# A longer row pitch for the activation tiles of a one-core transformer block kernel

## The chip, the cores and the metric

The kernel runs on one core of a Trainium2 chip. The metric is device time in microseconds (us) of one execution, the median of several; lower is better.

## The reference

One layer of a block on 256 positions with width 2048, in float32. Only what shapes the kernel is kept here:

```python
z = x @ w_in[i] + b_in[i]                       # 2048 -> 6 x 2048: u, v, a, b, gate A, gate B
zu, zv, za, zb, zga, zgb = jnp.split(z, IN_SPLITS, axis=-1)
sg = spatial_gating(gelu(zu), gelu(zv), ...)    # layer norm of v, 8 groups, 128-position blocks
y_a = sg @ w_gm_out[i]
c = causal_depthwise_conv(za * sigmoid(zb), cv_w[i], cv_b[i])      # 31 taps
c = silu(layer_norm(c, ...)); y_b = c @ w_cv_out[i]
mix = (sigmoid(zga) * y_a + sigmoid(zgb) * y_b) @ w_o[i]
x = layer_norm(ALPHA * x + mix, ...)
idx, gate = peer_route(xf, peer_wq[i], peer_keys[i])     # 8 heads, top 16 of 128 x 128 keys
u = jnp.take(u_tab, ib, axis=0); h = einsum('tkd,td->tk', u, xb)   # 16384 experts
v = jnp.take(v_tab, ib, axis=0); y = einsum('tk,tkd->td', gb * gelu(h), v)
x = layer_norm(ALPHA * x + y, ...)
x = x + sigmoid(x @ ple_w_gate[i]) * (p[i] @ ple_w_proj[i])
```

## The kernel before

Every product is done by TensorE in a split form: a float32 operand is cut into a high part (`hi`, rounded to the type fp32r by ScalarE) and a low part (`lo`, the rest, made by VectorE), both in `split` (L101 to L103). Activations are kept split and transposed, contraction on the partitions: `xT`, `mT`, `x1T` (one after another in the one buffer of pool `act`) and `sgT`, `cT` (pool `s32`) are tiles of 16 rows per partition, one row for each contraction tile `kt`. A row has 512 elements of 4 bytes, 2048 bytes: 256 high parts, then 256 low parts.

Weights come from memory as `raw` tiles of 128 x 1024 (512 KB, L131), in one fixed order, and are split into `hi` and `lo`. Two of them make a unit.

- `prod_t` (L147 to L171) is the product with the result transposed. The weights are stationary, and the row `x[:, kt, :]` streams as the moving operand. For each half of the contraction there are 8 matmuls of 512 columns with `hi` (L155) and 8 of 256 columns with `lo` (L159), each with a weight load of its own. It issues high 0 to 7 and low 0 to 7 for the first half, high 8 to 14, low 8 to 15 and high 15 for the second. So a unit is 32 matmuls in runs of 8 or 9 high, 8 low, 7 high, 8 low. It is called 80 times with `xT`, 16 with `sgT`, 16 with `cT`, 144 with `x1T` (16 for the router's queries, 128 for all experts' first layer).
- `prod_n` (L181 to L207) is the product with positions on the partitions. Here 128 columns of `x` are the stationary operand and 512 columns of `hi` or `lo` stream (L195). It runs with `xT` (v), `mT` (w_o) and `x2T` (last gate).
- The experts' second layer (L798) has `ahl`, the split activation of the experts, as stationary operand, and `hi` or `lo` streams, 512 columns each time.

All experts are computed densely, and the router's result is laid over them as a table of gates (L728). The order on each engine is the order in which the code is written, with VectorE's side work (convolution, norms, routing) taken from a queue `side` between halves of a unit.

Tiles get their places in order of allocation in pools, and `pad` tiles (L70 to L75) only take up room ahead of a pool. The byte offsets of the tiles inside a partition, as the built program has them, stand under the change.

Of the kernel before, what the change touches and what calls it, by code (L numbers as in the profile page):

```python
# [10 lines left out]
F32R = mybir.dt.float32r  # L11
# [5 lines left out]
P = 128  # L17
D = 2048
T = 256
KT = D // P  # L20
# [8 lines left out]
ALPHA = 2.0 ** 0.25  # L29
EPS = 1e-5  # L30
EARLY = 64
NEG = -3.0e38
RATES = {"ab": 3.1, "v": 3.0, "u": 3.6, "ga": 2.6, "wa": 3.0}
ROUTE_RATE = 1.0
# [4 lines left out]
def block_kernel(ctx: ExitStack, tc: tile.TileContext, a: dict, out: bass.AP):  # L39
    nc = tc.nc  # L40

    def pool(stack, name, bufs=1, **kw):
        return stack.enter_context(tc.tile_pool(name=name, bufs=bufs, **kw))
# [3 lines left out]
    const = pool(ctx, "const")  # L47
    sp = pool(ctx, "stream")
    ev = pool(ctx, "evac", bufs=2)
    act = pool(ctx, "act")  # L50
# [19 lines left out]
    def pad(p_, nbytes):  # L70

        t = p_.tile([P, nbytes // 4], F32, name="pad")
        nc.gpsimd.memset(t[:, 0:1], 0.0)

    pad(const, 608)  # L75

    class InOrder:

# [185 lines left out]
    pc = pool(pa, "pa_const")  # L264
    s32 = pool(pa, "s32", bufs=2)
    s16 = pool(pa, "s16", bufs=3)

    xT = act.tile([P, KT, 2 * T], F32R, tag="act", name="xT")
    def load_x(q):
        raw = sp.tile([P, 1024], F32, tag="raw", name="rawx", bufs=4)  # L270
        nc.sync.dma_start(raw, a["xT"][q])
        rv = raw.rearrange("p (k t) -> p k t", k=4)
        split(rv, xT[:, q * 4:q * 4 + 4, :T], xT[:, q * 4:q * 4 + 4, T:])
# [156 lines left out]
    cT = s32.tile([P, KT, 2 * T], F32R, tag="s32", name="cT")  # L430
    csum = pc.tile([P, T], F32, tag="cacc", name="csum", bufs=2)
    crs = pc.tile([P, T], F32, name="crs")
    pad(pc, 256)
    ct1 = pc.tile([P, T], F32, tag="cacc", name="ct1", bufs=2)
    Q = 4

# [56 lines left out]
    flush()  # L493


    mT = act.tile([P, KT, 2 * T], F32R, tag="act", name="mT")
    for ct in range(KT):
        ps = prod_t(cT)
        y = join_t(ps)
# [34 lines left out]
    ped = dram.tile([P, NB, D], F32, name="ped")  # L534
    with tc.issue_after(last_dma[0].ins):
        nc.sync.dma_start(ped, pe)
    x1T = act.tile([P, KT, 2 * T], F32R, tag="act", name="x1T")
    ln1.finish(x1T)
    x1d = dram.tile([P, NB, D], F32, name="x1d")
    with tc.issue_after(last_dma[0].ins):  # L540
# [6 lines left out]
    op_ = pool(pg, "oh", bufs=3)  # L547
    ga1 = pool(pg, "ga1").tile([P, EARLY, T], F32, name="ga1")
    pr = ctx.enter_context(ExitStack())
# [15 lines left out]
    def top8_first(vdst, idst, src, scr):  # L565
        paced.max(vdst[:, 0:8], src)
        paced.max_index(idst[:, 0:8], vdst[:, 0:8], src)
        paced.match_replace(scr, vdst[:, 0:8], src, NEG)

# [123 lines left out]
    def ga_parts(lo_, hi_):  # L693
        if lo_ < min(hi_, EARLY):
            yield ga1[:, lo_:min(hi_, EARLY), :], lo_
        if max(lo_, EARLY) < hi_:
            yield now["ga2"][:, max(lo_, EARLY) - EARLY:hi_ - EARLY, :], max(lo_, EARLY)

# [13 lines left out]
    while side:  # L712
        u_unit(i2, ROUTE_RATE)
        i2 += 1
    assert i2 <= EARLY
    pr.close()
# [209 lines left out]
```

## Time and profile before

| | us |
|---|---|
| median of 3 runs | 2523.0 (2522.11 to 2524.18) |
| the profiled execution, its time | 2522.61 |
| its span, first to last instruction | 2520.8 |
| TensorE (PE) busy | 2491.0 (99%) |
| weight loads (PEld) busy | 2143.3 (85%) |
| VectorE (DVE) busy | 1902.8 (75%) |
| ScalarE (ACT) busy | 1263.8 (50%) |

The profiled execution has 1.8 us outside its span, and is 0.4 us below the median. Matmuls overlap each other in the pipeline, so a matmul's own duration in a row is longer than the step from its start to the next one's start; where the text speaks of a matmul's step, it means the latter. Weight loads run beside the matmul ahead of them. The mean granted clock of TensorE was 0.998 of 2.4 GHz.

### The profile page before, as it was taken

The numbers are of one execution on the slowest core, as the hardware profiler recorded it, in microseconds if no ns is written. First come the engines' busy times: TensorE is split into PE (matmuls) and PEld (weight loads), VectorE is DVE, ScalarE is ACT, GpSimd is POOL, SyncE is SP. The second block draws the span as 40 slices with busy tenths as digits, with TensorE's granted clock in tenths as the row PEclk, the third lists the DMA queues.
The fourth block names the chain that finished last, engine by engine and source line by source line (L and its number), as shares of the span: only waits on it lengthen the run. The fifth ranks groups of instructions, "written<-read, shape, count | busy, mean of one in ns | idle before, by whom it ended". The sixth has DMA issues, their size and how long they took to land.

```text
span 2520.8 us, 35685 instructions
## 1 busy us (share of the span) xinstructions
PE 2491.0 (99%) x13178; PEld 2143.3 (85%) x13178; DVE 1902.8 (75%) x3550; ACT 1263.8 (50%) x1922; POOL 12.1 (0%) x16
## 2 busy tenths in 40 slices
PE   8999999999999999999999999999999999999989
PEld 7888888888888788888888888888888888888877
DVE  6999999999765689988777888755665565555585
ACT  5444555447543545455444444545555544555553
POOL 0000000000000000000000000000000000000000
PEclk9999999999999999999999999999999999999999
DMA  7656555556566655555554455557676666666655
GB/s 239 242 184 199 185 192 176 178 175 216 188 194 193 232 176 185 190 184 184 167 161 164 160 167 167 168 188 254 200 225 195 193 194 195 193 193 193 194 190 175
DMA packets 130335, 482.15 MB, mean 191 GB/s; under 512 B 14832, under 2 KB 15472, under 8 KB 128240
## 3 DMA queue, kind: packets, MB, share of 16 engines
q1 hardware_dynamic: 129024, 476.11, 58.9%
q10 hardware_dynamic: 1136, 3.76, 0.4%
q8 instruction: 103, 1.69, 0.3%
q14 instruction: 72, 0.59, 0.1%
HBM read 473.52 MB, written 6.29 MB: 190 GB/s over the span
## 4 chain that ended last, share of the span: by engine, by line
PE 94%; DVE 4%; ACT 1%; issue 1%; DMA 0%; POOL 0%; SPq 0%; DVEq 0%; POOLq 0%; ACTq 0%
PE pst L155 35%; PE py L798 27%; PE pst L159 18%; PE psn L195 10%; PE pgate L728 2%; DVE lo L103 2%; ACT hi L102 1%; DVE cacc L82 1%; PE ptr L249 0%; PE pss L606 0%; PE pmix L402 0%; DVE ct L446 0%; DMA rawx<-in_xT 0%; PE ppe L531 0%; DVE x1N L82 0%
## 5 line engine op out<-in xcount | busy, mean ns | idle before, releaser
L103 DVE TENSOR_TENSOR lo<-raw,hi 128x1024 fp32r<-128x1024 f32 x864 | 1056.8, 1224 | 428.6 <-ACT hi L102 423.3
L102 ACT ACTIVATE hi<-raw 128x1024 fp32r<-128x1024 f32 x868 | 917.7, 1058 | 559.4 <-PE py L798 336.4
L155 PE MATMUL pst<-x1T,hi 128*128 128x512 f32 x2304 | 603.1, 399 | 3.2 <-DVE x1T L103 2.6
L798 PE MATMUL py<-hi,ahl 128*128 128x512 f32 x2048 | 506.6, 389 | 0.0
L155 PEld LDWEIGHTS pst<-x1T,hi 128*128 128x128 f32 x2304 | 413.6, 189 | 75.8 <-DVE x1T L103 3.5
L798 PEld LDWEIGHTS py<-hi,ahl 128*128 128x128 f32 x2048 | 384.5, 188 | 79.7
L155 PE MATMUL pst<-xT,hi 128*128 128x512 f32 x1280 | 328.3, 396 | 9.2 <-ACT hi L102 8.1
L159 PEld LDWEIGHTS pst<-x1T,lo 128*128 128x128 f32 x2304 | 314.3, 190 | 23.8
L159 PE MATMUL pst<-x1T,lo 128*128 128x256 f32 x2304 | 321.1, 282 | 0.0
L155 PEld LDWEIGHTS pst<-xT,hi 128*128 128x128 f32 x1280 | 232.0, 190 | 51.5 <-ACT hi L102 8.7
L798 PE MATMUL py<-lo,ahl 128*128 128x512 f32 x1024 | 274.6, 389 | 0.0
L175 ACT ACTIVATE e<-pst 128x256 f32<-128x256 f32 x160 | 61.5, 384 | 356.1 <-PE pst L155 356.1
L798 PEld LDWEIGHTS py<-lo,ahl 128*128 128x128 f32 x1024 | 192.2, 188 | 40.1 <-DVE lo L103 0.3
L82 DVE SCALAR_TENSOR_TENSOR cacc<-glu,cvw,cacc 128x256 f32<-128x256 f32 x464 | 197.3, 479 | 0.0
L159 PEld LDWEIGHTS pst<-xT,lo 128*128 128x128 f32 x1280 | 175.0, 191 | 17.2 <-DVE lo L103 4.9
L159 PE MATMUL pst<-xT,lo 128*128 128x256 f32 x1280 | 179.7, 283 | 2.8 <-DVE lo L103 2.8
L178 DVE TENSOR_TENSOR z<-pst,e 128x256 f32<-128x256 f32 x224 | 93.9, 419 | 70.9 <-ACT e L175 70.5
L175 ACT ACTIVATE e<-pst,binT 128x256 f32<-128x256 f32 x80 | 37.8, 472 | 169.6 <-PE pst L155 165.9
L725 DVE TENSOR_SCALAR oh<-iota,T,TG 128x128 f32<-128x128 f32 x256 | 87.7, 343 | 44.6 <-PE pgate L728 44.6
L103 DVE TENSOR_TENSOR ahl<-ga,ahl 128x256 fp32r<-128x256 f32 x256 | 106.9, 418 | 0.2 <-ACT ahl L102 0.2
L102 ACT ACTIVATE ahl<-ga 128x256 fp32r<-128x256 f32 x256 | 102.1, 399 | 1.6 <-DVE ga L736 1.6
L728 PE MATMUL pgate<-oh 128*128 128x128 f32 x512 | 78.9, 274 | 0.0
(290 smaller groups left out, 1799.7 us busy)
## 6 DMA issues: line engine op xcount, KB each, us to landing
raw<-in_peer_u SPq DMA_DIRECT2D x256, 512.0 KB, 3.4
raw<-in_peer_v SPq DMA_DIRECT2D x256, 512.0 KB, 5.0
raw<-in_wa SPq DMA_DIRECT2D x32, 512.0 KB, 3.4
raw<-in_wb SPq DMA_DIRECT2D x32, 512.0 KB, 3.4
raw<-in_wv SPq DMA_DIRECT2D x32, 512.0 KB, 3.4
raw<-in_wu SPq DMA_DIRECT2D x32, 512.0 KB, 3.4
raw<-in_wga SPq DMA_DIRECT2D x32, 512.0 KB, 3.3
raw<-in_w_gm_out SPq DMA_DIRECT2D x32, 512.0 KB, 3.3
```

Source lines behind the costliest of these rows:

```text
L82: return lambda *args, **kw: tc.keep_in_program_order(op(*args, **kw))
L102: nc.scalar.activation(hi, src, AF.Copy)
L103: eng.tensor_tensor(lo, src, hi.bitcast(F32), op=OP.subtract)
L155: nc.tensor.matmul(ps, hi[:, k * P:(k + 1) * P], x[:, kt, :], start=(kt == 0), stop=(kt == KT - 1))
L159: nc.tensor.matmul(ps[:, T:], lo[:, k * P:(k + 1) * P], x[:, half * 8 + k, :T], start=False, stop=False)
L175: nc.scalar.activation(e1, ps[:, T:], AF.Identity, bias=bias)
L178: nc.vector.tensor_tensor(z, ps[:, :T], e1, op=OP.add)
L195: nc.tensor.matmul(ps[b], x[:, kt, j * T + b * P:j * T + (b + 1) * P], w[:, k * 512:(k + 1) * 512], start=(kt == 0 and not is_lo and j == ...
L725: nc.vector.tensor_scalar(oh[:, 0, :], iota, T1[:, t:t + 1], TG[:, t:t + 1], op0=OP.is_equal, op1=OP.mult)
L728: nc.tensor.matmul(now["ps"][:, j * P:(j + 1) * P], oh[:, 0, :], oh[:, 1, :], start=True, stop=True)
L798: nc.tensor.matmul(py[b][half * 2 + k], ahl[:, j * T + b * P:j * T + (b + 1) * P], w[:, k * 512:(k + 1) * 512], start=(i2 == 0 and not is_ ...
```

## The change

The tiles `xT` and `mT` get rows of 520 elements (2080 bytes) and `x1T` rows of 514 (2056 bytes); of each row the first 512 are used, through a slice. The pad ahead of the streaming pool shrinks by 512 bytes, so that the pool `act`, now 512 bytes larger, ends where it ended. The pad in `pc` shrinks by 224 bytes.

```diff
+PITCH = 2 * T + 8
...
-    pad(const, 608)
+    pad(const, 96)
...
-    xT = act.tile([P, KT, 2 * T], F32R, tag="act", name="xT")
+    xT = act.tile([P, KT, PITCH], F32R, tag="act", name="xT")[:, :, :2 * T]
...
-    pad(pc, 256)
+    pad(pc, 32)
...
-    mT = act.tile([P, KT, 2 * T], F32R, tag="act", name="mT")
+    mT = act.tile([P, KT, PITCH], F32R, tag="act", name="mT")[:, :, :2 * T]
...
-    x1T = act.tile([P, KT, 2 * T], F32R, tag="act", name="x1T")
+    x1T = act.tile([P, KT, 2 * T + 2], F32R, tag="act", name="x1T")[:, :, :2 * T]
```

No instruction is added, removed or moved: on all five engines the built programs have the same rows in the same order (TensorE 4131 rows of equal neighbours, VectorE 2932, ScalarE 1756, GpSimd 19, SyncE 83), and only the line numbers behind the new line are one higher. What differs is places, in bytes inside a partition:

| tile | before | after | modulo 512 before, after |
|---|---|---|---|
| `raw`, 4 buffers | 18432 + 4096 n | 17920 + 4096 n | 0, 0 |
| `hi`, `lo`, 2 buffers each; weights of step k at + 512 k | 34816 + 4096 n | 34304 + 4096 n | 0, 0 |
| `xT`, `mT` row kt | 55296 + 2048 kt | 54784 + 2080 kt | 0, 32 kt |
| `x1T` row kt | 55296 + 2048 kt | 54784 + 2056 kt | 0, 8 kt |
| `cT` row kt | 113664 + 2048 kt | 113440 + 2048 kt | 0, 288 |
| `sgT` row kt | 146432 + 2048 kt | 146208 + 2048 kt | 0, 288 |
| `ahl`, 3 buffers | 91648 + 2048 n | the same | 0, 0 |
| `x2T` row kt | 88064 + 2048 kt | the same | 0, 0 |

The tiles of `s16` (`vN`, `uT`, `sA`, `sB`, `zN`) move by 224 bytes like `sgT`; those of `evac` move by 512; `glu`, the expert tables and the routing tiles stay.

## Rows read from the trace of the kernel before

**Rows 1.** The page: the span, TensorE's busy time and its granted clock.
```profile
span 2520.8 us, 35685 instructions
...
PE 2491.0 (99%) x13178; PEld 2143.3 (85%) x13178; DVE 1902.8 (75%) x3550; ACT 1263.8 (50%) x1922; POOL 12.1 (0%) x16
...
PEclk9999999999999999999999999999999999999999
```

**Rows 2.** The chain of work that ended last, by engine and line.
```profile
PE 94%; DVE 4%; ACT 1%; issue 1%; DMA 0%; POOL 0%; SPq 0%; DVEq 0%; POOLq 0%; ACTq 0%
```

**Rows 3.** Waits of TensorE, the longest: us in total, times, longest.
```profile
PE pst L155 <- ACT hi L102: 8.7, 4, 7.0
PE ptr L249 <- DVE x1N L241: 6.3, 1, 6.3
```

**Rows 4.** Groups of TensorE by line and shape: busy us, mean ns, idle before.
```profile
L155 PE MATMUL pst<-x1T,hi 128*128 128x512 f32 x2304 | 603.1, 399 | 3.2 <-DVE x1T L103 2.6 <-ACT hi L102 0.6
L798 PE MATMUL py<-hi,ahl 128*128 128x512 f32 x2048 | 506.6, 389 | 0.0
L155 PE MATMUL pst<-xT,hi 128*128 128x512 f32 x1280 | 328.3, 396 | 9.2 <-ACT hi L102 8.1 <-DVE xT L103 1.1
L159 PE MATMUL pst<-x1T,lo 128*128 128x256 f32 x2304 | 321.1, 282 | 0.0
...
L159 PE MATMUL pst<-xT,lo 128*128 128x256 f32 x1280 | 179.7, 283 | 2.8 <-DVE lo L103 2.8
...
L155 PE MATMUL pst<-sgT,hi 128*128 128x512 f32 x256 | 64.4, 393 | 0.0
...
L195 PE MATMUL psn<-hi,xT 128*128 128x512 f32 x256 | 63.2, 389 | 0.0
```

**Rows 5.** Timeline of TensorE, one unit with `x1T`: start us, us.
```profile
1031.59 1.12 PE L159 MATMUL pst<-x1T,lo 128*128 128x256 f32 x8
1032.55 1.78 PE L155 MATMUL pst<-x1T,hi 128*128 128x512 f32 x7
1034.16 1.11 PE L159 MATMUL pst<-x1T,lo 128*128 128x256 f32 x8
1035.11 2.23 PE L155 MATMUL pst<-x1T,hi 128*128 128x512 f32 x9
1037.18 1.11 PE L159 MATMUL pst<-x1T,lo 128*128 128x256 f32 x8
```

**Rows 6.** Timeline of TensorE in the experts' second layer.
```profile
1800.03 1.07 PE L798 MATMUL py<-lo,ahl 128*128 128x512 f32 x4
1800.94 1.98 PE L798 MATMUL py<-hi,ahl 128*128 128x512 f32 x8
1802.75 1.07 PE L798 MATMUL py<-lo,ahl 128*128 128x512 f32 x4
```

**Rows 7.** Single lines of the kernel: duration ns min/median/max, first and last start us.
```profile
L159 PE MATMUL pst<-sgT,lo x256: 277/283/283, 465.6 to 552.8; 128*128 128x256 f32 x128
...
L155 PE MATMUL pst<-cT,hi x256: 389/391/398, 649.2 to 738.3; 128*128 128x512 f32 x128
```

**Rows 8.** Timeline of weight loads, one that follows a wait, then the next.
```profile
832.97 0.19 PEld L531 LDWEIGHTS ppe<-lo,pT 128*128 128x128 f32 x1 [0.37 <-DVE lo L103]
833.08 0.19 PEld L532 LDWEIGHTS ppe<-hi,pT 128*128 128x128 f32 x1
```

**Rows 9.** Timeline of TensorE, low runs with `xT`, then with `sgT`.
```profile
52.80 1.12 PE L159 MATMUL pst<-xT,lo 128*128 128x256 f32 x8
...
58.39 1.12 PE L159 MATMUL pst<-xT,lo 128*128 128x256 f32 x8
...
521.51 1.12 PE L159 MATMUL pst<-sgT,lo 128*128 128x256 f32 x8
...
527.10 1.11 PE L159 MATMUL pst<-sgT,lo 128*128 128x256 f32 x8
```

**Rows 10.** Busy us by stretch: PE, PEld, DVE, ACT, POOL; clock, DMA share, GB/s.
```profile
290.00:550.00 260.00, 260.00 (x1513) 229.52 (x1512) 250.36 (x472) 132.86 (x192) 0.00 (x0) 1.00 0.57 184
```

## The prediction

> **What bounds the kernel now.** The page comes first: TensorE is busy for 2491.0 of 2520.8 us, at its upper clock level of 2.4 GHz in every slice [rows 1]. The chain of waits agrees: 94% of what ended last is TensorE's own work [rows 2]. Its waits are few, the longest two 8.7 and 6.3 us in total [rows 3]. So it is no wait that matters, but the step of each matmul. I read it from starts in the timeline, since durations hold a tail that overlaps the next matmul.
>
> In the experts' second layer the 12 matmuls from 1800.03 to 1802.75 take 2.72 us, 0.2267 each [rows 6]. Their 512 columns alone are 512 / 2.4 = 213.3 ns, so each has 13.4 ns more. Their duration is 389 ns [rows 4], so duration less step is 162. With this tail a `prod_t` unit can be read:
> - A unit with `x1T` goes from 1031.59 to 1037.18, 5.59 us [rows 5]. Its columns are 16 x 213.3 + 16 x 106.7 ns = 5.12.
> - Eight low matmuls take 0.96 us (1031.59 to 1032.55), 0.119 to 0.120 each, again some 13 ns above the columns. The shortest low matmul with `sgT` lasts 277 ns and the median 283 [rows 7]: a step of 114 occurs, and 120 is the rule.
> - Seven high ones take 1.61 and nine 2.07 us, 0.230 each, 3 to 4 ns above rows 6. By duration it is 393 with `sgT` against 389 (the means with `x1T` and `xT`, 399 and 396, also hold waits and long steps behind other work) [rows 4], and 398 at most with `cT` [rows 7].
>
> A weight load that follows a wait lets the next one start after 0.11 us (832.97 to 833.08) [rows 8]. In the low runs, where a load runs beside every stream of 256 columns, the step is 0.12. So the loads and the streams of the one engine seem to cost each other some nanoseconds, and how many depends on how they fall. That is where a place in memory could matter.
>
> **The change, part by part.** No instruction is added or moved, so every term is a price per matmul.
>
> *Rows of `xT` and `x1T` as moving operand.* 80 + 144 = 224 units, 3584 high and 3584 low matmuls, 1280 and 2304 of each [rows 4]. Before, each stream starts at the same place of the 512-byte grid as each weight block. After, it starts 32 kt bytes past it, or 8 kt with `x1T`. Bounds by the nearest rows:
> - Gain: high matmuls at the second layer's step, 393 - 389 = 4 ns x 3584 = 14.3 us, and low ones at the short step, 282.5 - 277 = 5.5 ns x 3584 = 19.7 us. Together 34 us.
> - Far end of a gain: the 13.4 ns go altogether, 224 x (5.59 - 5.12) = 105 us. No row shows a matmul near its columns alone, so I don't count on it.
> - Loss: all high ones at 398 instead of 393, 5 ns x 3584 = 17.9 us. A low one has no row far above 283 to go to.
>
> I take half of the 34 us, 17. The low run keeps its 120 after the first matmul because every pair of a stream and a load starts alike, and with the pitch no two neighbours do. I expect a mix of the steps that are seen today (114 to 120, 227 to 236), not the best of them throughout.
>
> *`xT` and `mT` as stationary operand in `prod_n`.* 768 matmuls at 389 ns, as the group with `xT` shows [rows 4], already at the second layer's step. Zero; bounds are -13.4 and +9 ns (398 - 389) each, -10 to +7 us.
>
> *`sgT` and `cT`.* Their place goes from 0 to 288 in the grid, their pitch stays. `sgT` begins 1024 past a multiple of 2048 and `xT` at one, and both have the same unit, 527.10 - 521.51 and 58.39 - 52.80, 5.59 us each [rows 9]. But both lie alike on the 512 grid, so this doesn't settle what 288 does. 32 units, from -32 x 0.15 = -5 to +2.6 us (5 ns x 512); I take zero.
>
> *All else that moves.* `raw`, `hi`, `lo` and the evacuation tiles move by 512, a whole step of the grid; `ahl` and `x2T` stay. The second layer and the last gate I leave as they are: zero. ScalarE and VectorE read and write rows as long as before, and where their own steps changed by some ns it would be hidden under TensorE. The tightest cover is from 290 to 550 us, where VectorE is busy for 250.4 of 260 us [rows 10]: 9.6 us could be gained there before it becomes the bound. My 17 us are 17 / 224 = 0.076 per unit, and about 40 units fall there (260 / 5.59 = 46, less those with `sgT`), at most 3.5 us. The cover holds. What is late next is nothing new: if TensorE steps faster, each `raw` must come 1.4% sooner, and DMA is busy for 0.57 there.
>
> *The pads* are one element written on GpSimd, as before. Zero.
>
> Sum on the profiled execution: 2522.6 (span 2520.8 and 1.8 around it) - 17 = 2505.6. The median lies 0.4 above that execution, so 2506.
>
> **Two rules of the Trainium skill.** The Trainium skill, "SBUF — State Buffer", section "Who interferes with whom", speaks against the change: TensorE has two read ports, one for the stream and one for weight loads, independent of each other, and "PE and ACT never wait on anyone". By that rule alone the pitch does nothing, which is the second case below. The trace here doesn't quite agree with it: a load steps in 0.11 us alone and in 0.12 beside short streams [rows 5, 8].
>
> The Trainium skill, "TensorE: Matmul & The Clock Gate", section "Wait — 56ns, not 53.3ns?", gives 215.7 ns for 512 warm columns in another type, a fixed extra of about 2.5 ns. The row here has 13.4 [rows 6]. If places in memory made the whole difference, an estimate by that page is 11 ns x 7168 = 79 us; the row decides, and the figure is in no bound.
>
> **The rivals.**
>
> *The place doesn't matter.* The extra of a matmul may be fixed, and the pattern (short first low step, longer high steps behind a low run) an effect of the order alone. For it: `xT`, `sgT` and `x1T` have the same 5.59 us; the extra is 13 ns for 256 as for 512 columns. Against it: steps of equal matmuls differ by up to 9 ns with nothing to wait for. Time 2523, within 2518 to 2528.
>
> *Slower: the streams fall into the long step.* The high matmuls that come just behind a low run show up to 398 ns, and runs of the second layer, which are undisturbed, settle at 389. If a start that shifts from row to row keeps them from settling, all 3584 stay at 398: +17.9 us, 2541. It decides once the mean over the 7168 matmuls rises by 0.7 ns (5 us). The 8-byte pitch is the more exposed, as a row of `x1T` no longer starts on a whole multiple of 16 bytes for odd kt. For this rival: the settling itself, a high run behind low ones needs several matmuls. Against it: low runs do worse settled (120) than fresh (114), so unsettling must help these.
>
> *The full gain.* Both steps go to the shortest seen, `sgT` and `cT` too: 34 + 5 us, 2484.
>
> **How the numbers follow.** 0.2% is 5 us, about what a measurement of this kernel can tell from no change. A partial gain, 6 to 30 us, 2493 to 2517: 0.48. The full gain or more: 0.08. No change: 0.24. Slower: 0.20, half of it between 2528 and 2538, the rest up to 2550. So faster 0.56, same 0.24, slower 0.20. The time is that of the likeliest, 2506, whose own range is 2493 to 2517. The range for 8 in 10 leaves out most of the full gain and half of the slower case: 2484 to 2537.
>
> **What would show it.** In the changed kernel the same rows tell: low runs of 8 with `x1T` and `xT` under 0.95 us, median durations under 283; high ones at 389 to 393; a unit of 5.51 instead of 5.59 us. `prod_n` and the second layer unchanged at 389, and 2.72 us for 12. If units stay at 5.59, the place doesn't matter. If high ones show 396 and more, it is the slower rival. I would be wrong in kind if the second layer, whose operands keep their places on the grid, changed its step, or if TensorE began to wait for `lo` or `z` from VectorE between 290 and 550 us.

## The result and the profile after

The changed kernel takes 2542.13 us (median of 3 runs, 2538.81 to 2542.5) against 2523.0: a ratio of 1.0072, 95% interval 1.0049 to 1.0094. The change costs 19 us. The forecast was a gain of 17; the time lies above its range and where the rival "the streams fall into the long step" had put it (2541).

The page of the changed kernel, the span and the busy time of each engine:

```profile
span 2540.4 us, 35685 instructions
...
PE 2511.2 (99%) x13178; PEld 2147.3 (85%) x13178; DVE 1903.8 (75%) x3550; ACT 1263.7 (50%) x1922; POOL 12.1 (0%) x16
```

The span grew by 19.6 us and TensorE's busy time by 20.2 [rows 1]; VectorE, ScalarE and GpSimd stayed within 1 us. So TensorE's own work became longer. Its waits did not; the two longest, in us in total, times and longest one:

```profile
PE pst L156 <- ACT hi L103: 8.9, 4, 7.4
...
PE ptr L250 <- DVE x1N L242: 6.3, 1, 6.3
```

In total they are those of [rows 3] within 0.2 us. The tight stretch from 290 to 550 us has not turned into a wait for VectorE either (columns as in [rows 10]):

```profile
290.00:550.00 260.00, 260.00 (x1501) 227.27 (x1500) 248.25 (x472) 132.67 (x192) 0.00 (x0) 1.00 0.56 182
```

Twelve matmuls fewer fit into it, at the same granted clock of 1.00. Where the time went is told by the groups by line and shape (busy us and mean ns, then idle):

```profile
L156 PE MATMUL pst<-x1T,hi 128*128 128x512 f32 x2304 | 609.1, 401 | 3.2 <-DVE x1T L104 2.6 <-ACT hi L103 0.6
L799 PE MATMUL py<-hi,ahl 128*128 128x512 f32 x2048 | 506.6, 389 | 0.0
...
L156 PE MATMUL pst<-xT,hi 128*128 128x512 f32 x1280 | 333.1, 400 | 9.2 <-ACT hi L103 8.3 <-DVE xT L104 0.9
L160 PE MATMUL pst<-x1T,lo 128*128 128x256 f32 x2304 | 324.6, 283 | 0.0
...
L160 PE MATMUL pst<-xT,lo 128*128 128x256 f32 x1280 | 180.8, 284 | 2.4 <-DVE lo L104 2.2
...
L156 PE MATMUL pst<-sgT,hi 128*128 128x512 f32 x256 | 65.2, 395 | 0.0
L196 PE MATMUL psn<-hi,mT 128*128 128x512 f32 x256 | 65.1, 395 | 0.7 <-ACT hi L103 0.7
L196 PE MATMUL psn<-hi,xT 128*128 128x512 f32 x256 | 64.7, 394 | 0.0
L196 PE MATMUL psn<-hi,x2T 128*128 128x512 f32 x256 | 63.7, 390 | 0.0
...
L160 PE MATMUL pst<-sgT,lo 128*128 128x256 f32 x256 | 35.1, 279 | 0.0
```

Every group of 512 columns whose operands moved on the grid has a longer mean than in [rows 4]: high matmuls with `xT` 400 for 396, with `x1T` 401 for 399, with `sgT` 395 for 393, `prod_n` with `xT` 394 for 389. Low matmuls are longer by 1 ns with `xT` and `x1T`, and shorter with `sgT` (279 for 282). The second layer (`py`), whose places on the grid did not move, stays at 389. The timeline of TensorE shows it for one unit with `x1T`, and for 12 matmuls of the second layer:

```profile
1043.73 1.10 PE L160 MATMUL pst<-x1T,lo 128*128 128x256 f32 x8
1044.67 1.81 PE L156 MATMUL pst<-x1T,hi 128*128 128x512 f32 x7
1046.32 1.15 PE L160 MATMUL pst<-x1T,lo 128*128 128x256 f32 x8
1047.31 2.24 PE L156 MATMUL pst<-x1T,hi 128*128 128x512 f32 x9
1049.38 0.87 PE L160 MATMUL pst<-x1T,lo 128*128 128x256 f32 x6
...
1830.04 1.07 PE L799 MATMUL py<-lo,ahl 128*128 128x512 f32 x4
1830.95 1.98 PE L799 MATMUL py<-hi,ahl 128*128 128x512 f32 x8
1832.76 1.07 PE L799 MATMUL py<-lo,ahl 128*128 128x512 f32 x4
```

The unit goes from 1043.73 to 1049.38: 5.65 us for 5.59 [rows 5]. Its first eight low matmuls take 0.94 us (0.96 before), the second eight 0.99 (0.95), the seven high ones 1.65 (1.61). The 12 of the second layer take 2.72 us as before [rows 6]. Durations hold the tail that overlaps the next matmul, so the account is made from starts: for each group the sum of (start of the next matmul less its own start) over the whole trace.

| group | before, us | after, us | difference |
|---|---|---|---|
| `prod_t` with `x1T`, high and low | 822.7 | 831.9 | +9.2 |
| `prod_t` with `xT`, high and low | 458.3 | 463.3 | +5.0 |
| `prod_n` with `xT` and `mT` | 175.2 | 179.5 | +4.3 |
| `prod_t` with `sgT` and `cT` | 178.9 | 179.5 | +0.6 |
| second layer, high and low | 703.0 | 703.0 | 0 |

These make 19.1 of the 19.6 us. Not all of it comes from places: this execution has one stretch more at the lower clock level of 1.2 GHz than that of the kernel before, 3.4 us long, in a unit with `xT`. TensorE had waited 1.83 us for `lo` just before it (timeline, then the stretch with columns as in [rows 10]):

```profile
571.87 2.02 PE L160 MATMUL pst<-xT,lo 128*128 128x256 f32 x8 [1.83 <-DVE lo L104]
573.69 3.04 PE L156 MATMUL pst<-xT,hi 128*128 128x512 f32 x9
576.57 1.11 PE L160 MATMUL pst<-xT,lo 128*128 128x256 f32 x8
...
572.00:575.40 3.40, 3.40 (x13) 3.02 (x14) 1.71 (x3) 1.04 (x2) 0.00 (x0) 0.51 0.71 243
```

These 17 matmuls take 4.70 us instead of some 3.05, so about 1.7 of the 5.0 us of `xT` are the clock's.

By shape, the mean step of the high matmuls rose from 237.8 to 240.2 ns (`x1T`) and 237.6 to 240.8 (`xT`); that of the low ones, which were to fall, rose as well, from 119.2 to 120.9 and 120.4 to 121.2 (all with the long steps behind other work in them, those of `xT` also with the 1.2 GHz stretch, which makes 0.6 ns of the one rise and 0.7 of the other). In the changed kernel the step of a given row is nearly the same in every unit: with `x1T`, row 14 (at 112 bytes) has 260 ns in 141 of 142 units, for 226 to 236 in most units before; row 0 (at 0 bytes) has 226 where no other work comes between, and low rows lie from 113 to 131. It is a pattern that belongs to the order of the places. Row 14 of one unit, and the low matmul that follows it:

```profile
1108.17 0.43 PE L156 MATMUL pst<-x1T,hi 128*128 128x512 f32 x1
1108.43 0.41 PE L160 MATMUL pst<-x1T,lo 128*128 128x256 f32 x2
```

### The profile page after: what moved, and what is told of

The parts are those of the page before. It is cut to its first block, busy times and chain, and to the rows that moved or that the text cites. A ratio compares the mean times of both kernels' runs of the same rounds, so it can differ in the third digit from the quotient of the medians.

```text
span 2540.4 us, 35685 instructions
## 1 busy us (share of the span) xinstructions
PE 2511.2 (99%) x13178; PEld 2147.3 (85%) x13178; DVE 1903.8 (75%) x3550; ACT 1263.7 (50%) x1922; POOL 12.1 (0%) x16
## 4 chain that ended last, share of the span: by engine, by line
PE 94%; DVE 4%; ACT 1%; issue 1%; DMA 0%; POOL 0%; SPq 0%; DVEq 0%; ACTq 0%; POOLq 0%
PE pst L156 35%; PE py L799 27%; PE pst L160 18%; PE psn L196 10%; PE pgate L729 2%; DVE lo L104 2%; ACT hi L103 1%; DVE cacc L83 1%; PE ptr L250 0%; PE pss L607 0%; PE pmix L403 0%; DVE ct L447 0%; DMA rawx<-in_xT 0%; PE ppe L532 0%; DVE x1N L83 0%
```

## The experiments

The theory after the result: the step of a matmul depends on where its moving row lies relative to the weight block that is loaded beside it, and the pitch replaces one good place by many (sixteen with `x1T`, eight modulo 256 with `xT`), most of them worse. The first rival: the pitch is innocent, and the moved tiles (`hi`, `lo`, `sgT`, `raw`, 512 or 224 bytes elsewhere) cost the time.

**The change in parts.** Three kernels keep every place and pad of the changed kernel, and undo the pitch of some rows.

`xT` and `mT` keep 2080 bytes, `x1T` has 2048 again:

```diff
-    x1T = act.tile([P, KT, 2 * T + 2], F32R, tag="act", name="x1T")[:, :, :2 * T]
+    x1T = act.tile([P, KT, 2 * T], F32R, tag="act", name="x1T")
```

> The changed kernel with x1T back at rows of 2048 bytes; xT and mT keep 2080. Theory (each pitched operand pays by its own matmuls): the matmuls with x1T give back 831.9 - 822.7 = 9.2 us of start-to-start steps, the rest stays, so about 2533, 10 above the kernel before. Rival (the moved places of all other tiles cost, not the rows): about 2542 as in the changed kernel. Second rival (only the 8-byte pitch costs): 2523.

Only `x1T` keeps its pitch (2056):

```diff
-    xT = act.tile([P, KT, PITCH], F32R, tag="act", name="xT")[:, :, :2 * T]
+    xT = act.tile([P, KT, 2 * T], F32R, tag="act", name="xT")
...
-    mT = act.tile([P, KT, PITCH], F32R, tag="act", name="mT")[:, :, :2 * T]
+    mT = act.tile([P, KT * 2 * T + 128], F32R, tag="act", name="mT")[:, :KT * 2 * T].rearrange("p (k t) -> p k t", k=KT)
```

(`mT` is allocated 512 bytes longer, so that the pool stays as large.)

> The changed kernel with xT and mT back at rows of 2048 bytes; x1T keeps 2056. Theory: prod_t with xT gives back 5.0 us, prod_n with xT and mT 2.2 + 2.0 us; x1T's 9.2 and 0.6 of sgT and cT stay: about 2533. Rival (moved places of all other tiles): 2542. Second rival (only the 8-byte pitch costs): 2542 as well, with prod_t on xT at 5.59 us a unit.

All rows at 2048, the places of the changed kernel, as against the kernel before (`mT` again 512 bytes longer):

```diff
-    pad(const, 608)
+    pad(const, 96)
...
-    pad(pc, 256)
+    pad(pc, 32)
...
-    mT = act.tile([P, KT, 2 * T], F32R, tag="act", name="mT")
+    mT = act.tile([P, KT * 2 * T + 128], F32R, tag="act", name="mT")[:, :KT * 2 * T].rearrange("p (k t) -> p k t", k=KT)
```

> The changed kernel's pads and its longer buffer, but all rows at 2048 bytes: tiles lie where the change puts them (raw, hi, lo, xT 512 lower, sgT and cT at 288 past the 512 grid), no row is pitched. Theory: only sgT and cT pay, 0.6 us in 32 units (high 234, low 117 ns): 2523 to 2524, units with xT and x1T back at 5.59 us. Rival (moved places cost): 2542.

| rows with a pitch | us, median (lowest to highest, runs) | ratio to before (95%) |
|---|---|---|
| `xT`, `mT` | 2531.14 (2530.73 to 2533.12, 6) | 1.0033 (1.0021 to 1.0046) |
| `x1T` | 2533.61 (2532.91 to 2534.32, 5) | 1.0040 (1.0026 to 1.0053) |
| none | 2524.37 (2523.02 to 2526.23, 11) | 1.0004 (0.9995 to 1.0013) |

The kernel before had 2523.59 beside them (16 runs). With all rows at 2048 the time is that of before, so the moved places are innocent. Over that kernel the pitch of `xT` and `mT` costs 6.8 us and that of `x1T` 9.2, together 16 of the 19. For `x1T` that is what the steps gave; for `xT` and `mT` they gave 5.0 + 4.3, or 7.6 without the 1.2 GHz stretch. The execution with the pitch of `xT` and `mT` alone has no such stretch there, and its steps with `xT` add up to 461.6 us, 3.3 above the kernel before. The groups by line say it again; with the pitch of `xT` and `mT` alone:

```profile
L156 PE MATMUL pst<-x1T,hi 128*128 128x512 f32 x2304 | 602.8, 398 | 3.3 <-DVE x1T L104 2.6 <-ACT hi L103 0.6
...
L156 PE MATMUL pst<-xT,hi 128*128 128x512 f32 x1280 | 332.1, 399 | 9.2 <-ACT hi L103 8.2 <-DVE xT L104 1.0
...
L196 PE MATMUL psn<-hi,mT 128*128 128x512 f32 x256 | 65.1, 395 | 0.6 <-ACT hi L103 0.6
```

and with that of `x1T` alone:

```profile
L156 PE MATMUL pst<-x1T,hi 128*128 128x512 f32 x2304 | 610.4, 402 | 3.2 <-DVE x1T L104 2.6 <-ACT hi L103 0.6
...
L196 PE MATMUL psn<-hi,mT 128*128 128x512 f32 x256 | 63.7, 390 | 0.8 <-ACT hi L103 0.8
```

Each pitch lengthens its own matmuls and no others: `x1T` is at 398 without and 402 with it, `prod_n` with `mT` as stationary operand at 390 without and 395 with it.

**A constant shift, on either operand or both.** The experts' two layers repeat the same matmuls hundreds of times. In one kernel their moving rows are read s bytes further, s = 8 (i2 mod 64), so the product is no longer the reference's; all 16 rows of a unit have the same s. In the second layer both halves of the columns are read at the same s. Weight blocks stay.

```diff
+            return flat[:, kt * 2 * T + sm:kt * 2 * T + sm + n]
...
-                nc.tensor.matmul(ps, hi[:, k * P:(k + 1) * P], x[:, kt, :],
+                nc.tensor.matmul(ps, hi[:, at(k):at(k) + P], row(kt, 2 * T),
...
+        sh = 2 * (i2 % 64)
+        ps = prod_t(x1T, n_side, sh, 0, x1F)
...
-                             w[:, k * 512:(k + 1) * 512],
+                             w[:, sm:sm + 512],
```

> The kernel before, streaming pool 512 lower. In the experts' first layer unit i2 reads its moving rows 8 x (i2 mod 64) bytes further on, and in the second layer each i2 reads hi and lo as the moving operand that much further on; the weights stay. It computes with shifted data in both layers, so it isn't the reference's product; the instructions are the same in number and shape. Theory (the step follows the place of the stream against the weights that are loaded beside it): at shift 0 units of 5.59 us and second-layer steps of 226.7 ns; at other shifts the steps differ and repeat for the same shift, at 288 bytes high 234 and low 117 ns in a unit. Second layer at other shifts above 227, around 229 to 236. Rival (it is the change of place from one matmul to the next that costs, a constant shift is free): 5.59 us and 226.7 at every shift.

It took 2548.94 us (one run). In the second layer 12 matmuls share a shift. The timeline of TensorE there, at 232, 240, 248 and 256 bytes, eight high and four low each:

```profile
1807.39 2.04 PE L813 MATMUL py<-hi,ahl 128*128 128x512 f32 x8
1809.28 1.09 PE L813 MATMUL py<-lo,ahl 128*128 128x512 f32 x4
1810.21 2.05 PE L813 MATMUL py<-hi,ahl 128*128 128x512 f32 x8
1812.09 1.11 PE L813 MATMUL py<-lo,ahl 128*128 128x512 f32 x4
1813.04 2.00 PE L813 MATMUL py<-hi,ahl 128*128 128x512 f32 x8
1814.88 1.08 PE L813 MATMUL py<-lo,ahl 128*128 128x512 f32 x4
1815.80 2.00 PE L813 MATMUL py<-hi,ahl 128*128 128x512 f32 x8
1817.64 1.07 PE L813 MATMUL py<-lo,ahl 128*128 128x512 f32 x4
```

At 240 bytes the 12 take 2.83 us (1810.21 to 1813.04). From start to start, their steps are 228, 234, 239, 234, 239 ns and so on. At 256 bytes they are 230, 236, 228, 232, 231, 227, 227, 226, 227, 227, 226, 227, those of no shift: it settles at 227. At 64 bytes a cycle of 226, 229, 232 stays, at 192 one of 231 and 236. Each shift keeps to a cycle of its own, or to one constant step (230 ns at 104 bytes, 240 at 120); all repeat after 256 bytes, and no mean is below 227. In the first layer, with 16 high and 16 low matmuls in runs, means of the steps over both units of a shift, without those behind other work (a unit is 16 times the sum of both):

| shift, bytes | 0 | 16 | 64 | 120 | 136 | 192 | 256 | 320 |
|---|---|---|---|---|---|---|---|---|
| high, ns | 230.1 | 231.7 | 229.7 | 236.1 | 238.0 | 233.0 | 231.5 | 229.5 |
| low, ns | 118.0 | 117.0 | 116.8 | 120.6 | 120.7 | 115.0 | 118.2 | 116.8 |
| unit, us | 5.57 | 5.58 | 5.544 | 5.707 | 5.739 | 5.567 | 5.595 | 5.541 |

The columns 0 and 256, the same place modulo 256, differ by 0.025 us: so much the units scatter. Low matmuls do gain at many places, as the forecast had it; high ones lose more at most. 64 bytes is best. At 288 bytes the steps are 233.3 and 117.3 ns, as expected from `sgT`.

The rival, that the change of place from one matmul to the next costs and a constant shift is free, fell in its second half. But a change does count as well: in a unit with all rows at 112 bytes row 14 has 225 to 230 ns, not the 260 that it has in the changed kernel, where row 13 lies at 104. In the shifted kernel 260 comes up both times that the first matmul of a unit at 112 (modulo 256) follows directly on a unit at 104, once from 1025.57 to the next start at 1025.83:

```profile
1025.57 0.43 PE L164 MATMUL pst<-x1T,hi 128*128 128x512 f32 x1
1025.83 0.41 PE L164 MATMUL pst<-x1T,hi 128*128 128x512 f32 x1
```

In the second layer the same change of the shift gives 230, so what ran before counts too.

Then the same shift on the weight blocks alone, and on both:

```diff
+            return k * P + sw - (P if k == 7 and sw else 0)
...
+        ps = prod_t(x1T, n_side, 0, sh, x1F)
...
+            sm, sw = 0, sh
+            c = j * T + b * P + sw - (P if j == 1 and b == 1 and sw else 0)
```

> As the shifted-stream kernel, but now the weights are read 8 x (i2 mod 64) bytes further on and the streams stay (in the first layer hi and lo, in the second ahl), so both layers compute with shifted data. Theory (only the difference of the two places counts, modulo 256 bytes): a load shift of s gives what a stream shift of 256 - s gave: at 192 high 229.8 and low 116.8 in the first layer and the cycle 226, 229, 232 in the second; at 64 the second layer goes 231, 236 by turns; at 0 and 256 it settles at 227. Rival (the place of the stream alone counts): 5.59 us a unit and 227 at every load shift.

```diff
+        ps = prod_t(x1T, n_side, sh, sh, x1F)
...
+            sm, sw = sh, sh
```

> Streams and weights shifted alike, 8 x (i2 mod 64) bytes, in both layers, which compute with shifted data. Theory (only the difference counts): the second layer settles at 227 and units of the first take 5.59 us at every shift; the whole run is near 2523. Rival (each place counts by itself, as against a fixed grid): the steps change with the shift as in the shifted-stream kernel, run near 2549.

2542.51 and 2543.27 us (one run each; the kernel before beside these and the next two: 2520.74, one run). Blocks shifted by 192 give the cycle 226, 229, 232 that streams had at 64; blocks shifted by 64 give 231, 236, that of streams at 192. So, at multiples of 32 bytes, what counts in the second layer is the difference of both places, modulo 256. In the first, blocks at 192 have 229.4 and 117.9 ns, where streams at 64 had 229.7 and 116.8: the high step came as expected, the low one not. With both shifted alike by a multiple of 32 the second layer settles at 227, as the theory wanted. But with both shifted by an odd multiple of 16 it settles at 233 and 234, and by odd multiples of 8 it cycles at means of 231 and 233: the difference alone does not decide there, and the theory's 2523 for this kernel was wrong. Nor is an equal place the only one with 227: with blocks at 120 bytes and streams on the grid the second layer settles there as well.

**High and low apart.** In the first layer the stream lies a bytes past the high blocks, in steps of 32, and b past the low ones, in steps of 16; in the second `hi` lies a and `lo` b bytes past the blocks, in steps of 16; all pairs, but for two of the second layer:

```diff
+        ps = prod_t(x1T, n_side, -8 * (i2 // 16) % 64, -4 * (i2 % 16) % 64)
...
+            sm = 4 * (i2 // 16 + 8 * half) if is_lo else 4 * (i2 % 16)
```

> Weights hi and lo read at shifts of their own: in the first layer the stream lies 32 x (i2 div 16) bytes past hi and 16 x (i2 mod 16) past lo, in the second hi and lo lie at all 256 pairs of 16-byte shifts past ahl; both layers compute with shifted data. Theory (the step follows the difference of stream and the load beside it, each kind by its own difference): with hi at 0 or 64 and lo at 192 units fall to about 16 x 230 + 16 x 115 ns = 5.52 us, under the 5.59 of today; in the second layer no pair goes below the 227 of (0, 0). Rival (one difference for both kinds is what counts, or the run before decides more than the place): lo's own shift changes a unit by less than 0.03 us.

2543.4 us (one run). A first-layer unit has 5.574 us at (a, b) = (0, 0), 5.518 at (64, 64), 5.531 at (64, 192), 5.539 at (0, 192) and 5.670 at (160, 112), one unit each. The place of the low operand alone moves a unit by up to 0.1 us, more than the rival allowed; no mixture is better than 64 for both. In the second layer no pair is clearly below (0, 0), which has 228.3 ns a matmul, the settling in it: the others have 228.2 to 236.

**Is it the load that takes the time?** If the 13.4 ns that a matmul has above its columns were taken by the weight load beside it, a narrower load would take less. In the second layer, 64 and then 32 of the 128 columns are loaded (and 64 or 32 rows written) for a quarter of the i2 each:

```diff
+            W = (P, 64, 32, P)[i2 // 32]
+            c = j * T + b * P
+            nc.tensor.matmul(py[b][half * 2 + k][:W, :], ahl[:, c:c + W],
```

> The kernel before, but for i2 from 32 to 63 the second layer's matmuls load 64 columns of weights and from 64 to 95 32, and write as many rows of the result; it leaves that part of the product out. Theory (the 13.4 ns over the columns are what the load beside the stream takes from it): the step falls with the width of the load, 227 ns at 128, about 220 at 64 and 217 at 32. Rival (13.4 ns are the stream's own, a fixed price of 512 columns): 227 at every width.

2530.02 us (one run). The groups by line and shape:

```profile
L800 PE MATMUL py<-hi,ahl 128*128 128x512 f32 x1024 | 253.8, 389 | 0.0
...
L800 PE MATMUL py<-hi,ahl 128*32 128x512 f32 x512 | 128.9, 394 | 0.0
...
L800 PE MATMUL py<-hi,ahl 128*64 128x512 f32 x512 | 128.4, 393 | 0.0
```

The mean grows from 389 to 393 and 394, the step from 226.7 to 230.0 and 231.7 ns, again in cycles (236, 229, 225, 226, 234, 230 at 64). A narrower load, longer steps: the theory of stolen time fell, and so did the rival of a fixed 227. My reading is that the step depends on how load and stream fall together in time, and that a shorter load shifts that as another place does; no run shows it directly.

**The better place, in the whole kernel.** The kernel before, with rows of 2048 bytes, and `xT`, `x1T`, `sgT`, `cT` 64 bytes past the grid; `mT`, `ahl` and `x2T` stay on it:

```diff
-    xT = act.tile([P, KT, 2 * T], F32R, tag="act", name="xT")
+    xT = act.tile([P, KT * 2 * T + 16], F32R, tag="act", name="xT")[:, 16:].rearrange(
+        "p (k t) -> p k t", k=KT)
...
-    pad(tabs, 256)
+    pad(tabs, 192)
...
+    pad(tp, 192)
```

(`x1T` as `xT`.)

> The kernel before with rows of 2048 bytes, but xT, x1T, sgT and cT lie 64 bytes past the 256-byte grid on which hi and lo lie; mT, ahl and x2T stay on it. It computes the whole reference. Theory (the difference of stream and load modulo 256 sets the steps): a prod_t unit goes from 5.59 to 5.52 to 5.55 us, as the shifted reads showed at 64, over 256 units -11 to -17 us; prod_n with xT, whose loads now lie at 64, goes from 227 to 233 ns over 384 matmuls, +2.5 us. Sum 2509 to 2515, faster by 0.3 to 0.6%. Rival (only the mean step of a shifted read changes, and the neighbours' waits take it back): 2523.

And with `xT` left on the grid, since it is also loaded in `prod_n`:

> As the kernel with rows at 64, but xT stays on the grid: x1T, sgT and cT alone lie at 64, and the whole reference is computed. Theory: 176 units x 0.042 to 0.07 us = -7 to -12 us, prod_n with xT at 227 ns as before: 2511 to 2516. Against the other kernel it tells whether xT's 80 units (-3.4 to -5.6) outweigh the 2.5 us of its loads. Rival: 2523.

2514.77 us (2514.14 to 2516.06, 6 runs), ratio 0.9968 (0.9956 to 0.9980); and 2514.86 (2513.72 to 2516.53, 6 runs), ratio 0.9967 (0.9955 to 0.9979). The kernel before had 2522.91 beside them (11 runs). Both times lie in the ranges that were expected, the first at the upper end. The timeline of a unit with `x1T`, `xT` moved too:

```profile
1024.07 1.10 PE L159 MATMUL pst<-x1T,lo 128*128 128x256 f32 x8
1025.01 2.23 PE L155 MATMUL pst<-x1T,hi 128*128 128x512 f32 x9
1027.08 1.07 PE L159 MATMUL pst<-x1T,lo 128*128 128x256 f32 x8
1027.99 1.76 PE L155 MATMUL pst<-x1T,hi 128*128 128x512 f32 x7
1029.59 1.10 PE L159 MATMUL pst<-x1T,lo 128*128 128x256 f32 x8
```

5.52 us instead of 5.59: the unit that the forecast wanted (5.51), from a constant offset. The groups of the same kernel show who gains:

```profile
L159 PE MATMUL pst<-x1T,lo 128*128 128x256 f32 x2304 | 316.1, 279 | 0.0
...
L159 PE MATMUL pst<-xT,lo 128*128 128x256 f32 x1280 | 175.8, 279 | 3.2 <-DVE lo L103 3.2
...
L195 PE MATMUL psn<-hi,xT 128*128 128x512 f32 x256 | 64.9, 395 | 0.0
```

and of the one with `xT` on the grid:

```profile
L159 PE MATMUL pst<-xT,lo 128*128 128x256 f32 x1280 | 179.9, 284 | 2.9 <-DVE lo L103 2.9
...
L195 PE MATMUL psn<-hi,xT 128*128 128x512 f32 x256 | 63.3, 389 | 0.0
```

Low matmuls go from 282 and 283 [rows 4] to 279. `xT` at 64 wins as moving operand about what it loses as stationary one (395 for 389), so both kernels have the same time.

## Why the prediction was wrong

- **What bounds the kernel**: right. TensorE's steps are the time, and what changed is in them: 19.1 of 19.6 us stand in the table of steps. One reading was too smooth: a slice of the page at 9 tenths can hide a short stretch at 1.2 GHz, and one more of these makes 1.7 of the 19.6 us.
- "*Rows of `xT` and `x1T` as moving operand*", -17: this step failed. It measured +14.2 (9.2 and 5.0), 12.5 without the 1.2 GHz stretch. The reason given, that a low run keeps 120 ns because stream and load start alike and any other place mixes in shorter steps, holds for some places (115.0 to 117.0 at 16, 64 and 192 bytes) and not for others (120.6 at 120). Under the pitch the low steps went up by 1.7 ns (`x1T`) and, without the 1.2 GHz stretch, 0.1 (`xT`) on the mean instead of down. And the high matmuls were counted as a gain, though [rows 4] showed the second layer, with every pair of a stream and a load alike, at the shortest mean of all. That row said that the old place is the good one for a run of wide matmuls; I read it as the step of an undisturbed run, whatever its place. The shifted kernels show that no place has a mean below its 227 ns.
- Constant shifts explain part of the 12.5 us. Over the multiples of 32 bytes, which the rows of `xT` take, the shifted unit has 5.604 us on the mean, 0.014 above 5.59; over 0 to 120 in steps of 8, the places of `x1T`, 5.632, 0.042 above. That makes an estimate of 80 x 0.014 + 144 x 0.042 = 7.2 us. The rest, some 5 us, is then left to places that change from one matmul to the next. Row 14 of `x1T` shows such a change at work: 260 ns for some 228 at a constant 112 bytes are 4.6 us over 144 units. But other rows come out shorter than at a constant place (row 0 has 226 for 236), so this one row is not the account of the rest, which stays open.
- "*`xT` and `mT` as stationary operand in `prod_n`*", zero: mis-sized. It measured +4.3, inside its bounds (-10 to +7). Their step went from 226.7 to 232.4 ns, as the difference of the places also counts when the pitch is on the loaded side.
- "*`sgT` and `cT`*", zero: +0.6, inside the bounds. Their offset of 288 is 32 modulo 256; high steps rose from 230.3 to 233.6 and low ones fell from 119.1 to 117.1.
- "*All else that moves*" and the pads, zero: right, by the kernel with the moved places alone (1.0004) and the second layer's 703.0 us. The cover from 290 to 550 us held; it had nothing to hide. The working counts about 40 units there, but 46 less the 16 with `sgT`, which start between 463 and 553 us, is about 30, so its 3.5 us would have been 2.3; nothing hangs on it.
- **The rivals.** "*The streams fall into the long step*" came out, by its own point of decision: the mean of the 7168 matmuls had to rise by 0.7 ns, and it rose by 12.5 us / 7168 = 1.7. Its picture was half right. High steps do not settle where the place changes, but they rose by some 2.5 ns and not by 5 each, and the remaining microseconds came from low matmuls, `prod_n` and the 1.2 GHz stretch, which it did not count. So that its 2541 lies so near the measured time is in part luck. Its argument against itself, that unsettling must help low runs, was the same error as the forecast's. "*The place doesn't matter*" is refuted by the three kernels with parts of the change; "*the full gain*" too, though a constant offset of 64 bytes reaches its unit.

The rule of the Trainium skill, "SBUF — State Buffer", section "Who interferes with whom", by which the two read ports of TensorE are independent, gives no difference between any of these kernels. The runs do not bear it out as far as time goes: the same matmuls step by 226.7 to 240 ns as one operand moves by some bytes; whether the ports are what they share, no run shows. The fixed extra of about 2.5 ns that the Trainium skill, "TensorE: Matmul & The Clock Gate", section "Wait — 56ns, not 53.3ns?", gives for another type was reached at no place: the smallest mean step of 512 columns here stayed at 226.7.

What stays open: why both operands at an odd multiple of 16 bytes settle at 233 instead of 227 and blocks at 120 bytes at 227, what a change of place costs, why 64 bytes suits the runs of low matmuls, and what the 13.4 ns above the columns are, since a narrower load does not lower them.

## What to carry to other kernels

Where TensorE's steps are the bound, the place of the moving row relative to the weight block loaded beside it is worth some per cent of a step: rows with a common place (a pitch that is a multiple of 256 bytes) keep to that place's cycle, and a pitch that walks through many places meets the worse ones too, and the changes between them, which here cost 0.7%. For runs of 512 columns alone nothing tried was clearly better than both operands on the 256-byte grid; for runs that mix 512 and 256 columns an offset of 64 bytes was the best, and it costs only a pad (-0.32%). A group that already shows the shortest step of the kernel is evidence for its layout: ask what its operands' places are before moving the others away from them.

## What the runs showed of the hardware

- The step of equal matmuls without any wait depends on the operands' places in the partition, with a period of 256 bytes: 227 ns (both on the grid) up to a mean of 240 (stream at 120 bytes) for 512 columns, and means from 115.0 to 121.7 over the shifts of the stream for 256. Most places show a cycle of a few steps that repeats within 1 ns, at each pass over the same shift.
- At multiples of 32 bytes the same difference modulo 256 (stream at 64, or block at 192) gives the same cycle within a nanosecond, in runs of 512 columns.
- Places that change from one matmul to the next give steps that no constant place here shows: 260 ns at 112 bytes behind 104.
- Loading 64 or 32 weight columns instead of 128, and writing as many rows, lengthens the step beside it, from 226.7 to 230.0 and 231.7 ns.
